# Odd mixer: three neighbouring pairs of steps change places in the order that TensorE follows

## Chip, cores and metric

The kernel runs on one core of a Trainium2 chip. The metric is the device time of one execution in microseconds (us), here the median of several executions. A profiled execution of the same kernel gives the trace from which all rows below come.

## What is computed

The reference is a two-layer network over 256 tokens of width 1024. Each layer has a gated feed-forward block, a mixer, a second feed-forward block and a gated per-layer embedding. The change concerns the mixer of the second layer, which the program calls `mix1`, the odd mixer:

```
x_gate, x_rg, u = split_cols(xn @ w_in, [512, 512, 512])
y_c = rg_lru_branch(x_gate, x_rg, ...)      # gated linear recurrence
y_d = s5_branch(u, ...)                     # state-space branch
h   = h + concatenate([y_c, y_d], axis=-1) @ w_out

rg_lru: xc = conv4(x_rg); r, i = sigmoid of two block-diagonal products of xc
        scan of (a, bx) over the tokens, times gelu(x_gate)
s5:     bu = B u;  x = complex scan of bu;  y = gelu(C x + d u)
        y * sigmoid(y @ w_glu + b_glu)
```

Everything is float32. Large products are made with three rounded matmuls (high x high, low x high, high x low), so that each weight tile is split into a rounded part `wh` and a rest `wl` before TensorE can use it.

## The kernel before

Activations are kept with features on the 128 partitions and the 256 tokens along the free axis. A projection of 1024 features into 128 is 8 steps of k with three matmuls each (lines 279, 280 and 281), 24 matmuls of 128x256, all into one PSUM tile `mm`. Weights come from DRAM through SyncE into `raw` tiles; ScalarE rounds them into `wh` (line 259), VectorE subtracts to get `wl` (line 260). `raw`, `wh` and `wl` have five buffers each, `mm` has five PSUM tiles, and `aux`, the PSUM tile of all small products, has three.

In the odd mixer a string, `ORDER`, lists steps by name and number. The program is written out step by step in that order, and TensorE (named PE in rows) executes its instructions in exactly this order (`manual_schedule` for PE). The instructions of VectorE (DVE), ScalarE (ACT), GpSimd (POOL) and SyncE (SP) are placed by a scheduler that follows from it. The steps that matter here:

- `r0` to `r3`: projections of the recurrence's input, 24 matmuls each. VectorE scales the result into `xr` (line 1205). `c` is the convolution (1212 on ScalarE, 1214 on VectorE), `b` its two gates (1224).
- `m0` to `m3`: matrices of one quarter of the S5 branch. Four transposes (line 1133) go into one `aux` tile, four more into a second, ScalarE copies both into `BT` (1134); then eight small products (1141) go into a third `aux` tile, `pk`, which VectorE (1142) and copies on both engines (1147) empty into `KT`.
- `s0` to `s3`: the states. Eight products (1157, tile `aux`) of the regrouped input `u4` (copied by both engines, line 1200) with `BT`; VectorE then works through lines 1160, 1161, 1163, 1164, two scans (1169), 1174, 1175, 1176 and 1177, which leave `XS`.
- `o0` to `o3`: the outputs. Products of `XS` and `u4` (1185, 1186) into one `aux` tile, which ScalarE empties with four Gelu activations (1188) into `us`.
- `z0`, `z2`: the product with `w_glu` (24 matmuls on tiles `BT`), then sigmoid on ScalarE (1265), a product on VectorE (1267), and a split of the result by ScalarE (304, `xhB`) and VectorE (305, `xlB`). `z0` gives parts 4 and 5 of the mixer's output `y`, `z2` parts 6 and 7.
- `p0` to `p3`: the first halves of four output projections, 12 matmuls each over parts 0 to 3 of `y`. The other halves, over parts 4 to 7, follow in `out_proj` directly behind the last step, beginning with output 0.

```
            steps = dict(
                s=s5_states, o=s5_out, m=s5_mats,
                r=lambda t: projected(xr[:, t, 3:], "r", t),
...
                z=glu,
                u=lambda q: self.ple_up(1, q),
                p=lambda j: self.out_first(y, j, ODD_HALF),
            )
            for st in ORDER.split():
                steps[st[0]](int(st[1:] or 0))
            self.out_proj(y, nxt, buf)
```

Of the kernel before, what the change touches and what calls it, by code (L numbers as in the profile page):

```python
# [61 lines left out]
CST = {}  # L62
M_SIDE = 1
F_SIDE = 16
ORDER = "r0 m0 s0 r1 m1 s1 o0 r2 m2 c0 o1 c1 r3 c2 c3 m3 b0 g0 b1 s2 b2 b3 s3 d g1 g2 g3 o2 e0 o3 y0 y2 e2 u0 h2 h0 f u1 z0 p0 p1 z2 p2 p3"
ODD_HALF = 0
RC_ENG = "vector"
EVEN_ORDER = "a x w0 w1 X Q0 d Q2 k Q4 Q6 K0 w2 V K2 e s0 q0 q1 l0 t0 w3 t1 l1 v0 t2 v1 t3 s4 v2 q2 o0 v3 o1 t4 q3 t5 t6 t7 v4 v5 u0 v6 v7 g y0 y2 u1 p0 p1 p2 p3"
# [140 lines left out]
class Kernel:  # L209
# [896 lines left out]
    def mix_odd(self, nxt, buf):  # L1106
# [6 lines left out]
        with ExitStack() as ctx:  # L1113
# [167 lines left out]
            )  # L1281
            for st in ORDER.split():
                steps[st[0]](int(st[1:] or 0))
# [118 lines left out]
```

## Time and profile before

| what | value |
|---|---|
| median of 3 runs | 1023.68 us (1023.31 to 1025.05) |
| the profiled execution's own time | 1031.07 us |
| its span from the first to the last instruction | 1029.3 us |
| mean granted TensorE clock over the span | 0.994 of full speed |
| busy: TensorE, VectorE, ScalarE, GpSimd | 98%, 73%, 56%, 5% of the span |

The profiled execution is 7.4 us longer than the median of the runs without a profile, and 1.8 us of it lie outside the span. The odd mixer stands at about 710 to 812 us of the span. In a row of a timeline the first number is the start from the beginning of the span, the second the busy time of all the instructions in the row; `[2.46 <-ACT BT L1134]` says that the engine stood idle for 2.46 us before it and what ended that. TensorE's starts are those at which matmuls issue: the busy time of a matmul overlaps the next one.

### The profile page before, as it was taken

The numbers are of one execution on the slowest core, as the hardware profiler recorded it, in microseconds if no ns is written. First come the engines' busy times: TensorE is split into PE (matmuls) and PEld (weight loads), VectorE is DVE, ScalarE is ACT, GpSimd is POOL, SyncE is SP. The second block draws the span as 40 slices with busy tenths as digits, with TensorE's granted clock in tenths as the row PEclk, the third lists the DMA queues.
The fourth block names the chain that finished last, engine by engine and source line by source line (L and its number), as shares of the span: only waits on it lengthen the run. The fifth ranks groups of instructions, "written<-read, shape, count | busy, mean of one in ns | idle before, by whom it ended". The sixth has DMA issues, their size and how long they took to land.

```text
span 1029.3 us, 21008 instructions
## 1 busy us (share of the span) xinstructions
PE 1009.5 (98%) x8526; PEld 994.3 (97%) x8526; DVE 753.1 (73%) x1350; ACT 571.4 (56%) x926; POOL 47.1 (5%) x134
## 2 busy tenths in 40 slices
PE   9999999999999999999999999999999999999996
PEld 8999999988899999999989999999898999999996
DVE  6877756589677777757689987876878777776665
ACT  7545445456565554546555764644678564545453
POOL 0000000200001000000240000002200000000000
PEclk9999999999999999999999999999899999999998
DMA  7655556465245655566446555564224565555641
GB/s 275 223 201 188 187 193 193 159 201 179 74 147 182 225 191 198 178 200 221 150 144 218 190 197 195 175 196 156 89 83 144 184 207 203 187 190 183 199 165 42
DMA packets 52945, 183.07 MB, mean 178 GB/s; under 512 B 5856, under 2 KB 6768, under 8 KB 52848
## 3 DMA queue, kind: packets, MB, share of 16 engines
q1 hardware_dynamic: 52160, 181.12, 52.7%
q8 instruction: 67, 1.10, 0.4%
q10 hardware_dynamic: 688, 0.61, 0.3%
q14 instruction: 30, 0.25, 0.1%
HBM read 180.13 MB, written 1.05 MB: 176 GB/s over the span
## 4 chain that ended last, share of the span: by engine, by line
PE 88%; DVE 6%; ACT 4%; issue 1%; DMA 1%; POOL 0%; SPq 0%; DVEq 0%; ACTq 0%; POOLq 0%
PE mm L279 26%; PE mm L281 26%; PE mm L280 26%; DVE wl L260 2%; ACT wh L259 1%; DMA h<-in_xT_dram 1%; PE mm L524 1%; PE mm L523 1%; PE mm L522 1%; PE mm L737 1%; PE mm L739 1%; PE mm L738 1%; PE aux L1141 0%; PE aux L1157 0%; PE aux L807 0%
## 5 line engine op out<-in xcount | busy, mean ns | idle before, releaser
L260 DVE TENSOR_TENSOR wl<-raw,wh 128x1024 fp32r<-128x1024 f32 (+2 forms) x350 | 414.8, 1190 | 152.0 <-ACT wh L259 151.4
L259 ACT CAST wh<-raw 128x1024 fp32r<-128x1024 f32 (+2 forms) x350 | 354.5, 1021 | 229.3 <-PE mm L280 108.0
L279 PE MATMUL mm<-xhA,wh 128*128 128x256 f32 x1200 | 331.8, 276 | 0.9 <-ACT xhA L322 0.9
L280 PE MATMUL mm<-xlA,wh 128*128 128x256 f32 x1200 | 332.0, 277 | 0.4
L281 PE MATMUL mm<-xhA,wl 128*128 128x256 f32 x1200 | 331.5, 276 | 0.0
L279 PEld LDWEIGHTS mm<-xhA,wh 128*128 128x128 f32 x1200 | 225.3, 188 | 1.6 <-ACT xhA L322 1.6
L280 PEld LDWEIGHTS mm<-xlA,wh 128*128 128x128 f32 x1200 | 225.3, 188 | 1.0 <-DVE xlA L323 1.0
L281 PEld LDWEIGHTS mm<-xhA,wl 128*128 128x128 f32 x1200 | 225.2, 188 | 0.2 <-DVE wl L260 0.2
L281 PE MATMUL mm<-gh,wl 128*128 128x256 f32 x704 | 195.2, 277 | 0.0
L279 PE MATMUL mm<-gh,wh 128*128 128x256 f32 x704 | 195.2, 277 | 0.0
L280 PE MATMUL mm<-gl,wh 128*128 128x256 f32 x704 | 195.2, 277 | 0.0
L281 PE MATMUL mm<-xhB,wl 128*128 128x256 f32 x576 | 162.1, 282 | 1.4 <-DVE wl L260 1.4
L279 PE MATMUL mm<-xhB,wh 128*128 128x256 f32 x576 | 162.6, 283 | 0.0
L280 PE MATMUL mm<-xlB,wh 128*128 128x256 f32 x576 | 162.2, 282 | 0.1
L281 PEld LDWEIGHTS mm<-gh,wl 128*128 128x128 f32 x704 | 132.9, 189 | 0.0
L280 PEld LDWEIGHTS mm<-gl,wh 128*128 128x128 f32 x704 | 132.1, 188 | 0.0
L279 PEld LDWEIGHTS mm<-gh,wh 128*128 128x128 f32 x704 | 132.1, 188 | 0.0
L281 PEld LDWEIGHTS mm<-xhB,wl 128*128 128x128 f32 x576 | 110.5, 192 | 1.7 <-DVE wl L260 1.6
L280 PEld LDWEIGHTS mm<-xlB,wh 128*128 128x128 f32 x576 | 109.4, 190 | 0.3 <-DVE xlB L305 0.3
L279 PEld LDWEIGHTS mm<-xhB,wh 128*128 128x128 f32 x576 | 109.2, 190 | 0.0
L304 ACT CAST gh<-s 128x256 fp32r<-128x256 f32 x88 | 35.4, 406 | 89.7 <-DVE s L416 89.7
L411 DVE TENSOR_TENSOR ab<-mm,R 128x512 f32<-128x512 f32 x82 | 56.4, 688 | 13.8 <-PE mm L281 12.6
(409 smaller groups left out, 1059.7 us busy)
## 6 DMA issues: line engine op xcount, KB each, us to landing
raw<-in_w_dram SPq DMA_DIRECT2D x309, 512.0 KB, 3.8
raw<-in_w_dram SPq DMA_DIRECT2D x36, 384.0 KB, 3.2
raw<-in_w_dram SPq DMA_DIRECT2D x4, 256.0 KB, 4.8
out_dram<-hg SPq DMA_DIRECT2D x4, 256.0 KB, 2.2
h<-in_xT_dram SPq DMA_DIRECT2D x2, 256.0 KB, 5.5
h<-in_xT_dram SPq DMA_DIRECT2D x1, 512.0 KB, 6.6
K<-kr ACTq DMA_DIRECT2D x2, 256.0 KB, 4.8
bd<-in_bd_dram SPq DMA_DIRECT2D x1, 512.0 KB, 4.6
```

Of the source, the lines that this page charges most:

```text
L259: nc.scalar.copy(wh[:, sl], raw[:, sl])
L260: self.last_split = nc.vector.tensor_sub(wl[:, sl], raw[:, sl], wh[:, sl].bitcast(F32))
L279: mm(out, wh, xh, start=start, stop=False)
L280: mm(out, wh, xl, start=False, stop=False)
L281: mm(out, wl, xh, start=False, stop=stop)
L304: self.nc.scalar.copy(hi, src)
L411: nc.vector.tensor_mul(ab, src[0].rearrange("p (t s) -> p t s", t=2), R[:, None, :].to_broadcast([P, 2, S]))
L522: mm(pt, a, wh, start=k == 0, stop=False)
L523: mm(pt, b, wh, start=False, stop=False)
L524: mm(pt, a, wl, start=False, stop=k == KD - 1)
L737: mm(pg[name][i], a, wh, start=k == 0, stop=False)
L738: mm(pg[name][i], b, wh, start=False, stop=False)
```

## The change

Three pairs of neighbours in `ORDER` change places: `s0 r1` becomes `r1 s0`, `o0 r2` becomes `r2 o0`, `z2 p2` becomes `p2 z2`.

```
-ORDER = "r0 m0 s0 r1 m1 s1 o0 r2 m2 c0 o1 c1 r3 c2 c3 m3 b0 g0 b1 s2 b2 b3 s3 d g1 g2 g3 o2 e0 o3 y0 y2 e2 u0 h2 h0 f u1 z0 p0 p1 z2 p2 p3"
+ORDER = "r0 m0 r1 s0 m1 s1 r2 o0 m2 c0 o1 c1 r3 c2 c3 m3 b0 g0 b1 s2 b2 b3 s3 d g1 g2 g3 o2 e0 o3 y0 y2 e2 u0 h2 h0 f u1 z0 p0 p1 p2 z2 p3"
```

No instruction is added or removed. TensorE's instructions move as blocks; those of the other engines move where the scheduler follows.

First place, TensorE behind `m0`. Before, these rows stand there (`aux_9416` is `m0`'s `pk`, `aux_9434` the tile of `s0`, `mm_9463` that of `r1`, `aux_9496` and `aux_9502` the two transposed tiles of `m1`; left out are further rows of the same tiles):

```order
L1141 MATMUL aux_9416<-cx_7221,xlA_7220 128x32
L1157 MATMUL aux_9434<-u_1376_9346,BT_9403 128x64 [waits DVE_49,Activation_49]
...
L279 MATMUL mm_9463<-xhB_8283,wh_9465 128x256
...
L1133 MATMUL aux_9496<-ident_76,xhA_7219 128x128 [waits PE_49]
...
L1133 MATMUL aux_9502<-ident_76,xlA_7220 128x128 [waits DVE_49,PE_49]
```

With the change (`aux_9466` is now the tile of `s0`, `mm_9434` that of `r1`):

```order
L1141 MATMUL aux_9416<-cx_7221,xlA_7220 128x32
L279 MATMUL mm_9434<-xhB_8283,wh_9436 128x256 [waits DVE_49,PE_49]
...
L1157 MATMUL aux_9466<-u_1376_9346,BT_9403 128x64 [waits DVE_49,Activation_49]
...
L1133 MATMUL aux_9496<-ident_76,xhA_7219 128x128 [waits PE_49]
...
L1133 MATMUL aux_9502<-ident_76,xlA_7220 128x128 [waits DVE_49,PE_49]
```

The projection `r1` has moved from behind `s0` to ahead of it, so that `m1` now follows `s0` directly. In the built program the second transposed tile of `m1` takes the PSUM bank that `s0` has just filled, and waits for VectorE's lines 1160 and 1161 to empty it. On VectorE these lines, with the emptying of `r1` ahead of them, stand as follows with the change:

```order
L260 TENSOR_TENSOR wl_9740<-raw_9738,wh_9739 128x1024 [waits DMAHW4_49,Activation_49]
L1205 TENSOR_TENSOR xr_9176<-mm_9434,R_9339 128x256 [waits PE_49]
L1147 COPY KT_1346_9172<-aux_9416 32x4x32 [waits Activation_49]
L1160 TENSOR_TENSOR ct_1399_9475<-aux_9466,rot_8648 128x512 [waits PE_49]
L1161 TENSOR_TENSOR ct_1400_9476<-aux_9466,rot_8648 128x512
```

Before, a third split of weights stood behind the one in the first row, and a copy of line 1147 between the last two rows; both have moved further down.

Second place, TensorE around `o0`. Before, `r2` (`mm_9572`) stood between `o0` (`aux_9555`) and `m2` (`aux_9605`, `aux_9611` and `pk` in `aux_9617`):

```order
L1186 MATMUL aux_9555<-u_1376_9346,KT_1346_9172 128x64
L279 MATMUL mm_9572<-xhB_8283,wh_9574 128x256
...
L1133 MATMUL aux_9605<-ident_76,xhA_7219 128x128 [waits DVE_49,PE_49]
...
L1133 MATMUL aux_9611<-ident_76,xlA_7220 128x128 [waits DVE_49,PE_49]
...
L1141 MATMUL aux_9617<-cx_7221,xhA_7219 128x32 [waits PE_49,Activation_49]
```

With the change `o0` is `aux_9587`, and `m2` follows it:

```order
L1186 MATMUL aux_9587<-u_1376_9346,KT_1346_9172 128x64
L1133 MATMUL aux_9605<-ident_76,xhA_7219 128x128 [waits DVE_49,PE_49]
...
L1133 MATMUL aux_9611<-ident_76,xlA_7220 128x128 [waits DVE_49,PE_49]
...
L1141 MATMUL aux_9617<-cx_7221,xhA_7219 128x32 [waits PE_49,Activation_49]
```

In both programs `pk` of `m2` takes the bank of `o0`, and its wait for ScalarE (`Activation_49`) is one for the Gelu activations of `o0`. What has moved is the projection between them.

Third place, ScalarE behind the epilogue of `z0`, with the change (`wh_10149` is the weight of `z2`, `wh_10192` that of `p3`, `wh_10287` that of output 4 in `out_proj`, `mm_10154` the tile of `z2`):

```order
L259 CAST wh_10149<-raw_10148 128x1024 [waits DMAHW7_49]
L259 CAST wh_10192<-raw_10191 128x1024 [waits DMAHW0_49]
L259 CAST wh_10287<-raw_10286 128x1024 [waits DMAHW1_49,DVE_49,PE_49]
L1265 ACTIVATE sq_10179<-mm_10154,cst_77 128x256 [waits PE_49]
L1265 ACTIVATE sq_10185<-mm_10154,cst_77 128x256
L304 CAST xhB_9369<-z_10181 128x256 [waits DVE_49]
```

Before, the rows stood in the same order, with the weight of `p2` in the first (the one of `z2` came earlier, in the place that `p2`'s has now). In both programs the third row waits until TensorE has done with the weight of `z2`, whose buffer it takes, and the sigmoids of `z2` stand behind it.

## Rows read from the trace of the kernel before

**Rows 1.** The page: each engine's busy time; the chain that ended last, by engine.

```profile
PE 1009.5 (98%) x8526; PEld 994.3 (97%) x8526; DVE 753.1 (73%) x1350; ACT 571.4 (56%) x926; POOL 47.1 (5%) x134
...
PE 88%; DVE 6%; ACT 4%; issue 1%; DMA 1%; POOL 0%; SPq 0%; DVEq 0%; ACTq 0%; POOLq 0%
```

**Rows 2.** TensorE's waits, whole span: us in total, times, longest.

```profile
PE aux L1157 <- ACT BT L1134: 2.5, 1, 2.5
PE mm L281 <- DVE wl L260: 2.2, 2, 1.4
```

**Rows 3.** Windows: length, then busy us (instructions) of PE, PEld, DVE, ACT, POOL, clock, DMA.

```profile
516.00:520.00 4.00, 2.66 (x24) 2.46 (x22) 4.00 (x9) 3.24 (x8) 1.00 (x1) 1.00 0.19 73
...
726.00:730.00 4.00, 3.74 (x18) 3.60 (x19) 3.09 (x5) 2.27 (x7) 2.87 (x1) 0.62 0.52 159
730.00:734.00 4.00, 4.00 (x22) 4.00 (x21) 3.53 (x8) 0.00 (x0) 0.40 (x1) 0.53 0.47 173
...
760.00:775.00 15.00, 15.00 (x128) 14.78 (x128) 14.68 (x26) 13.48 (x23) 1.45 (x3) 1.00 0.12 37
```

**Rows 4.** Timeline of TensorE, 726 to 746 us: `s0`, `r1`, `m1`, `s1`, `o0`, `r2`, `m2`.

```profile
726.21 3.55 PE L1157 MATMUL aux<-u,BT 128*128 128x64 f32 x16 [2.46 <-ACT BT L1134]
729.52 0.56 PE L279 MATMUL mm<-xhB,wh 128*128 128x256 f32 x1
...
734.34 0.60 PE L1133 MATMUL aux<-ident,xhA 128*128 128x128 f32 x4
...
736.91 1.98 PE L1157 MATMUL aux<-u,BT 128*128 128x64 f32 x16
738.73 0.61 PE L1185 MATMUL aux<-XS,cx 128*128 128x64 f32 x4
...
741.38 0.36 PE L279 MATMUL mm<-xhB,wh 128*128 128x256 f32 x1
...
744.29 0.60 PE L1133 MATMUL aux<-ident,xhA 128*128 128x128 f32 x4
...
745.16 0.31 PE L1141 MATMUL aux<-cx,xhA 128*128 128x32 f32 x2
```

**Rows 5.** Timeline of ScalarE, 725 to 745 us.

```profile
725.57 1.07 ACT L1134 COPY BT<-aux 128x512 f32<-128x512 f32 x2
...
741.65 1.28 ACT L1188 ACT_TABLE_LOAD   x1 [2.53 <-PE aux L1186]
742.95 1.54 ACT L1188 ACTIVATE us<-aux 32x256 f32<-32x256 f32 x4
```

**Rows 6.** Timeline of VectorE, 717 to 732 us.

```profile
717.91 2.36 DVE L260 TENSOR_TENSOR wl<-raw,wh 128x1024 fp32r<-128x1024 f32 x2 [1.32 <-ACT wh L259]
...
725.13 3.47 DVE L260 TENSOR_TENSOR wl<-raw,wh 128x1024 fp32r<-128x1024 f32 x3
...
729.80 0.69 DVE L1160 TENSOR_TENSOR ct<-aux,rot 128x512 f32<-128x512 f32 x1 [0.88 <-PE aux L1157]
...
730.60 0.68 DVE L1161 TENSOR_TENSOR ct<-aux,rot 128x512 f32<-128x512 f32 x1
```

**Rows 7.** Timeline of TensorE, 791 to 798 us: `z2`, then output 0.

```profile
791.20 0.38 PE L281 MATMUL mm<-BT,wl 128*128 128x256 f32 x1 [0.75 <-DVE wl L260]
...
793.77 0.28 PE L281 MATMUL mm<-BT,wl 128*128 128x256 f32 x1
...
797.76 0.39 PE L280 MATMUL mm<-xlB,wh 128*128 128x256 f32 x1
```

**Rows 8.** Timeline of ScalarE, 793 to 798 us.

```profile
793.97 1.05 ACT L259 CAST wh<-raw 128x1024 fp32r<-128x1024 f32 x1 [1.59 <-PE mm L280]
...
796.84 0.87 ACT L304 CAST xhB<-z 128x256 fp32r<-128x256 f32 x2 [1.08 <-DVE z L1267]
```

**Rows 9.** Timeline of VectorE, 791 to 798 us.

```profile
791.73 2.35 DVE L260 TENSOR_TENSOR wl<-raw,wh 128x1024 fp32r<-128x1024 f32 x2
795.05 1.23 DVE L260 TENSOR_TENSOR wl<-raw,wh 128x1024 fp32r<-128x1024 f32 x1 [0.97 <-ACT wh L259]
...
797.28 0.89 DVE L305 TENSOR_TENSOR xlB<-z,xhB 128x256 fp32r<-128x256 f32 x2
```

## Prediction

> **What bounds the kernel now.** I read the page first. TensorE is busy for 98% of the span and carries 88% of the chain that ended last [rows 1]. A change of order can therefore only win where TensorE stands still or runs slowly, and it loses where it makes TensorE wait. The list of TensorE's waits shows few: the longest of all is 2.5 us ahead of line 1157, behind ScalarE's copy of `BT` [rows 2], and this is the wait of `s0`. The windows of the granted clock come next: it is 0.62 in the mean from 726 to 730 us and 0.53 from 730 to 734 [rows 3], so TensorE ran at 1.2 in place of 2.4 GHz for about 7 us there, behind that wait. The timelines of the three engines around the three places give the durations. The reader is to see two things: a wait with a slow stretch behind it, which the first pair attacks, and three pieces of vector work (the emptying of `s0`, of `o0` and of `z2`) that lie under a projection now and do so no longer.
>
> **First pair, what it removes.** `s0` starts at 726.21 after 2.46 us of idle time, so `m0` ended at 723.75 [rows 4]. `r1` can start there: its weights are split at 717.91 + 2.36 = 720.27 [rows 6], in the same place on ScalarE and VectorE as before. A projection at full clock takes 744.29 - 741.38 = 2.91 us (`r2`), one at the low clock 734.34 - 729.52 = 4.82 us (`r1` now); the eight state products take 738.73 - 736.91 = 1.82 us (`s1`), those of `s0` now 729.52 - 726.21 = 3.31 [rows 4]. With the change `r1` runs from 723.75 to 726.66. `BT` is complete at 725.57 + 1.07 = 726.64 [rows 5], so `s0` follows at once and ends at 728.48. `m1` begins there and not at 734.34: 5.86 us earlier. Of these 2.46 are the wait, 1.49 + 1.91 = 3.40 the low clock, if the clock doesn't fall any more.
>
> **First pair, what it adds.** The second four transposes of `m1` need the bank of `s0`, so lines 1160 and 1161 must be done. Now `r1` lies between. VectorE began 1160 at 729.80, 0.28 us behind the start of the next matmul on TensorE, and the two lines take 0.69 and 0.68 [rows 4, 6]; the small copy between them moves behind. After the change that is 728.48 + 0.28 = 728.76 and an end at 730.13, or 0.1 sooner where the second begins before the first has written its last. VectorE is free by then: of its three splits from 725.13, 1.16 each, the third is moved away, so they end at 727.5, and the emptying of `r1` and a copy follow. The first transposes take half of 745.16 - 744.29 = 0.87 us [rows 4], so TensorE stands ready at 728.92 and waits **1.1 us** (1.0 to 1.3, the latter if the copy comes between all the same).
>
> **Second pair.** With `r2` ahead of it, `o0` stands 0.87 + 1.1 (the transposes and their wait) + 1.70 (the rest of `m1`, 736.91 - 734.34 - 0.87) + 1.82 (`s1`) + 2.91 (`r2`) = 8.4 us behind the end of `s0`; now it is 738.73 - 729.52 = 9.2 us without a wait [rows 4]. The move keeps that cover, and `o0`'s wait is 0 to 0.8 us; I take 0, since VectorE's chain from 1160 to `XS` has one wait on `r1` now that falls away. But `m2` loses its cover. Its `pk` needs the bank of `o0`, and ScalarE must first load the Gelu table and run four activations: they end at 742.95 + 1.54 = 744.49, which is 3.11 us behind the last of `o0` (741.38) [rows 4, 5]. Now `r2` fills that time. With the change only the eight transposes do, 0.87 us, so TensorE waits 2.2 us by the issue times; the first matmul of `r2` stands somewhat early in the model (its busy time is 0.36, that of the others 0.28), which takes 0.1 off: **2.1 us** (1.8 to 2.3). The table load starts only when `o0` is done (idle 2.53 us until then, released by line 1186 [rows 5]), so it cannot be hidden.
>
> A rule of the Trainium skill speaks against this pair more strongly: ScalarE: Activation LUTs, section What ACT_TABLE_LOAD costs, puts a switch to another set at 1283 ns and a drain of about 1380 ns. By it, which is an estimate from that page, the wait would be 2.1 + 1.4 = 3.5 us. The trace agrees with the load (1.28 us) but shows no drain behind it: the first Gelu starts 0.02 us after the load's end [rows 5]. The sum goes by the row.
>
> **Third pair.** `p2` comes into the place of `z2` and meets the same late split (0.75 us, [rows 7]): nothing changes there. `z2` follows twelve matmuls (half a projection, 1.45 us) later; its own `wl` is the first of the two at 791.73 and ready at 792.9 [rows 9], while `z2` needs it at 791.20 + 1.45 = 792.65: a wait of 0.25. The price lies behind `z2`. Its last matmul is at 793.77; then ScalarE splits the weight of output 4 (793.97), queued ahead of the sigmoids, VectorE does its half (795.05), and the split results come at 796.84 and 797.28, so that the matmul that needs part 6 starts at 797.76 [rows 7 to 9]. These 3.99 us hang on the end of `z2` alone. Now `p2`, `p3` and seven matmuls of output 0 cover all but 0.2 of it; with the change `p2` is gone from the cover, 1.45 us. Together **1.7 us** (1.4 to 1.9; ScalarE's and VectorE's order is the same, so nothing lets the sigmoids go first).
>
> **The sum.** 5.86 - 1.1 - 2.1 - 1.7 = 1.0 us earlier, and everything behind is a stream of matmuls that keeps the lead. By the bounds of these terms it is 0.4 (5.9 - 1.3 - 2.3 - 1.9) to 1.7 (5.9 - 1.0 - 1.8 - 1.4); a late `o0` would make it -0.4. The other queues cost nothing: SyncE's loads of `p2` and `z2` trade places under the three steps ahead of them, and GpSimd is busy for 5% [rows 1]. The profiled execution, 1031.07 us, would become 1030.1; the median of the runs is 7.4 us lower, and I assume that the difference carries over: 1023.68 - 1.0 = **1022.7**. A difference of 0.2%, 2.05 us, is about what can be told from none.
>
> **Rivals.**
> - The wait of `m2` makes the clock fall again (slower). For it: 2.1 us is close to the 2.46 us after which it fell, and what stands around both waits are small products and transposes. Against it: after the 1.4 us wait near 520 us [rows 2], with 1.34 us idle in its window, it stayed at 1.00 [rows 3]. It decides from a wait between 1.4 and 2.46 us on. Price, as for `s0` and `r1` now: 1.49 + 1.91 = 3.4 us, on `o1` and `r3`; 1023.68 - 1.0 + 3.4 = 1026.1, or 1024.4 if the low stretch is half as long. Chance 0.18.
> - The runs without a profile never had the slow stretch (slower). Only one execution shows it, and the three runs lie 1.7 us apart. Then 3.4 us of the saving don't exist: again 1026.1. Chance 0.13.
> - The third pair costs nothing, because output 0 can be kept busy or the splits come sooner than I follow them (faster): 1.0 + 1.7 = 2.7, so 1021.0. Against it: the order of ScalarE's rows. Chance 0.14.
> - VectorE becomes the bound: it is busy for 14.68 of the 15 us from 760 on [rows 3], and where it doesn't come earlier with TensorE, the lead of 2.7 is lost at `o3` and the third pair still costs 1.7: 1025.4. Against it: that full stretch begins behind `m3` and so moves with it. Chance 0.08.
> - The switch of the Gelu table holds ScalarE longer where TensorE waits for it. With as long again as the load itself, 1.28 us [rows 5], the sum is 1.0 - 1.3 = -0.3, so 1024.0. Against it: the row's activations follow the load at once. Chance 0.05. The page named above is what speaks for it.
>
> **How the numbers follow.** The forecast has 0.42 and its own range is 1021.9 to 1024.1. The range for 8 in 10 reaches from the free third pair, a little below (1020.6), to the two cases at 1026.1, a little above (1026.3); what is left out is a combination of two losses or a gain without any of the new waits. Faster by more than 0.2% (below 1021.63) is the free third pair and the edge of the forecast: 0.20. Slower (above 1025.73) is most of the first two rivals and some of the fourth: 0.26. The rest, 0.54, is within 0.2%.
>
> **What the profile of the changed kernel would show.** Right: no wait ahead of line 1157 at 726 us and a clock of 1.00 from 722 to 738; a wait of about 1.1 us ahead of the second transposes of `m1`, released by VectorE's 1161; one of about 2.1 us ahead of line 1141, released by ScalarE's 1188; `m3` about 2.7 us earlier than before; and about 1.6 us ahead of output 0's matmuls on parts 6 and 7, released by lines 304 and 305. Wrong: a clock of 0.5 anywhere from 730 to 750; no wait at 1141; output 0 running through; new waits at lines 1185 or 1224, which would be VectorE falling behind. The prediction fails as a whole if the slow stretch of before was not there in the timed runs, or comes back behind `m2`.

## The result, and the profile after

The changed kernel takes 1030.61 us (median of 7 runs, 1027.37 to 1032.68) against 1023.80 us of the kernel before beside it (7 runs, 1021.66 to 1025.50). The ratio is 1.0056 with a 95% interval of 1.0041 to 1.0070: slower by 0.56% (the medians lie 6.8 us apart), above the predicted range. Measured again beside other kernels it was 1029.82 against 1024.81, ratio 1.0056 (1.0035 to 1.0077).

The profiled execution of the changed kernel took 1027.37 us, its span is 1025.7. TensorE's waits over the whole span, to be held against [rows 2] (us in total, times, longest):

```profile
PE mm L281 <- DVE wl L260: 2.2, 2, 1.4
PE aux L1141 <- ACT us L1188: 2.1, 1, 2.1
...
PE mm L279 <- ACT xhB L304: 1.1, 1, 1.1
PE aux L1133 <- DVE ct L1161: 1.0, 1, 1.0
```

The 2.5 us ahead of line 1157 are gone, and three new waits stand there: `m2` behind the Gelus, output 0 behind the split of part 6, `m1` behind the emptying of `s0`. Where they stand is seen in TensorE's timeline, which answers to [rows 4] and [rows 7]:

```profile
721.20 2.14 PE L1157 MATMUL aux<-u,BT 128*128 128x64 f32 x16
...
724.82 0.63 PE L1133 MATMUL aux<-ident,xlA 128*128 128x128 f32 x4 [1.03 <-DVE ct L1161]
...
731.59 0.55 PE L1185 MATMUL aux<-XS,cx 128*128 128x64 f32 x4
...
734.21 0.61 PE L1133 MATMUL aux<-ident,xhA 128*128 128x128 f32 x4
...
737.34 0.41 PE L1141 MATMUL aux<-cx,xhA 128*128 128x32 f32 x2 [2.09 <-ACT us L1188]
...
739.15 0.87 PE L1185 MATMUL aux<-XS,cx 128*128 128x64 f32 x4
...
744.04 0.56 PE L279 MATMUL mm<-xhB,wh 128*128 128x256 f32 x1
...
747.89 0.60 PE L1133 MATMUL aux<-ident,xhA 128*128 128x128 f32 x4
...
794.63 0.38 PE L279 MATMUL mm<-xhB,wh 128*128 128x256 f32 x1 [1.12 <-ACT xhB L304]
```

`s0` starts without a wait, `o0` too. But behind the 2.09 us of `m2` everything becomes slow: `o1` takes 744.04 - 739.15 = 4.89 us, where `o0` took 734.21 - 731.59 = 2.62, and `r3` takes 747.89 - 744.04 = 3.85 us. The windows of the granted clock (length, then busy us and instructions of PE, PEld, DVE, ACT and POOL, the clock, the DMA share, GB/s) say why:

```profile
732.00:736.00 4.00, 3.25 (x30) 3.01 (x29) 4.00 (x9) 2.80 (x4) 1.73 (x3) 1.00 0.00 0
736.00:740.00 4.00, 2.66 (x21) 2.66 (x22) 1.40 (x5) 2.58 (x7) 0.26 (x2) 0.93 0.00 0
740.00:744.00 4.00, 4.00 (x21) 4.00 (x21) 3.84 (x10) 0.77 (x3) 0.83 (x2) 0.50 0.02 4
744.00:748.00 4.00, 4.00 (x28) 4.00 (x27) 1.17 (x2) 1.53 (x5) 0.04 (x1) 0.72 0.74 223
```

The clock is at 1.2 in place of 2.4 GHz for about 6.8 us ((0.07 + 0.50 + 0.28) x 4 / 0.5), as long as before behind the wait of `s0` [rows 3], some 12 us later in the span, or 18 us later in the mixer, which began 5.2 us earlier in this execution (line 387 ahead of it: 712.61 against 717.81 us). A second low stretch, of 3.4 us, stands at 258 us, in the even mixer, where no instruction was moved (two windows, same columns):

```profile
256.00:260.00 4.00, 4.00 (x26) 3.64 (x25) 2.16 (x5) 0.84 (x3) 0.00 (x0) 0.77 0.75 220
260.00:264.00 4.00, 4.00 (x20) 3.19 (x20) 0.79 (x2) 2.00 (x3) 0.00 (x0) 0.81 0.11 44
```

One more difference concerns the profile of before, not the change. In the second feed-forward block the same projection matmuls stood closer together in the changed kernel's execution. First before, then after, the same 60 us at full clock:

```profile
580.00:640.00 60.00, 60.00 (x512) 60.00 (x511) 49.21 (x89) 35.56 (x59) 0.00 (x0) 1.00 0.57 194
```

```profile
580.00:640.00 60.00, 60.00 (x532) 60.00 (x531) 51.02 (x97) 36.88 (x62) 0.00 (x0) 1.00 0.63 201
```

512 against 532 instructions: start to start 0.1178 against 0.1133 us. Summed over all projection matmuls, the slower step cost the profiled execution of before 9.6 us and that of after 1.3. These 8.3 us account for the 7.4 us by which the profile of before lay over its median.

### The profile page after: what moved, and what is told of

It reads as the page before. It is cut to its first block, busy times and chain, and to the rows that moved or that the text cites. A ratio compares the mean times of both kernels' runs of the same rounds, so it can differ in the third digit from the quotient of the medians.

```text
span 1025.7 us, 21005 instructions
## 1 busy us (share of the span) xinstructions
PE 1003.5 (98%) x8526; PEld 987.0 (96%) x8526; DVE 752.0 (73%) x1350; ACT 571.5 (56%) x926; POOL 45.9 (4%) x134
## 4 chain that ended last, share of the span: by engine, by line
PE 89%; DVE 6%; ACT 3%; issue 1%; DMA 1%; POOL 0%; SPq 0%; DVEq 0%; ACTq 0%; POOLq 0%
PE mm L279 26%; PE mm L281 26%; PE mm L280 26%; DVE wl L260 2%; ACT wh L259 1%; PE aux L1141 1%; DMA h<-in_xT_dram 1%; PE mm L524 1%; PE mm L522 1%; PE mm L523 1%; PE mm L737 1%; PE mm L739 1%; PE mm L738 1%; PE aux L1157 1%; PE aux L1185 0%
## 5 line engine op out<-in xcount | busy, mean ns | idle before, releaser
L281 PE MATMUL mm<-xhB,wl 128*128 128x256 f32 x576 | 159.8, 278 | 2.2 <-DVE wl L260 2.2
L279 PE MATMUL mm<-xhB,wh 128*128 128x256 f32 x576 | 160.3, 278 | 1.3 <-ACT xhB L304 1.1
L280 PE MATMUL mm<-xlB,wh 128*128 128x256 f32 x576 | 159.6, 277 | 0.1
```

Of the source, the lines that this page charges most:

```text
L279: mm(out, wh, xh, start=start, stop=False)
L280: mm(out, wh, xl, start=False, stop=False)
L281: mm(out, wl, xh, start=False, stop=stop)
```

## The experiments

Three theories. Theory 1: the time was lost inside the odd mixer, to the new waits and to a clock that falls behind them. Theory 2, its rival: it was lost in stretches that the change doesn't touch (258 us, the step of the matmuls). Theory 3 came out of the first four runs: the clock falls where little is computed, in the waits and in the small products around them. All runs are compared with the kernel before on the same chip: 1024.03 us for the first four, 1024.81 for the others.

**The kernel before, unchanged**, to see what differs between executions.

> The kernel before, unchanged, profiled a second time, because its first profile was 7.4 us longer than its median and shows two steps between matmuls in a row: 0.1133 us in most stretches, 0.118 us from 531 to 718 and from 784 to 826 us, 9.6 us in all. Theory 1 (the change costs what it does to the waits and the clock inside the odd mixer): median 1023 to 1025, and the slower step is chance: another stretch, or none, this time. Theory 2 (the times differ because of stretches that the change doesn't touch): the same program's own executions lie 5 us or more apart, and their clocks differ as those of the changed kernel did (0.988 to 0.992).

1025.53 us, ratio 1.0011 (0.9999 to 1.0023). Its profile has a low stretch behind `s0`'s wait again, but 3.4 us long and not 6.8. The slow step of the matmuls was there again (8.5 us), and it is in the profile of the first pair alone (8.8 us); the other ten profiles have 1.3 to 2.9 us of it. In these three most of it lies between 520 and 718 us, where no kernel here moves an instruction, so it isn't the change that brings it.

**The three pairs apart.** First pair:

```
-r0 m0 s0 r1 m1 s1 o0 r2 m2
+r0 m0 r1 s0 m1 s1 o0 r2 m2
```

> The first pair alone (r1 ahead of s0). Theory 1: 5.9 us saved at s0 and r1, 1.1 us lost at m1's second transposes and about 0.5 us ahead of o0, no wait of 2 us at m2 and so no fall of the clock in the mixer: 4 us under the kernel before, about 1019.7. Theory 2: no clear difference, within 2 us of the kernel before.

1025.21 us, ratio 1.0016 (1.0001 to 1.0031): a miss, since the pair that was to save most saved nothing. `s0`'s wait is gone, and the waits left are short (timeline of TensorE, `m1`, `o0` and `r2`):

```profile
731.63 0.63 PE L1133 MATMUL aux<-ident,xlA 128*128 128x128 f32 x4 [1.03 <-DVE ct L1161]
...
736.49 1.09 PE L1185 MATMUL aux<-XS,cx 128*128 128x64 f32 x4 [0.70 <-DVE XS L1176]
...
741.60 0.56 PE L279 MATMUL mm<-xhB,wh 128*128 128x256 f32 x1
...
746.70 0.60 PE L1133 MATMUL aux<-ident,xhA 128*128 128x128 f32 x4
```

Yet `o0` takes 5.11 us and `r2` 5.10: the clock is 0.53 from 736 to 740 us, 0.50 from 740 to 744 and 0.69 from 744 to 748, a low stretch of 10.2 us, longer than the one that was removed. This execution is the slowest of the twelve (1032.74 us; it has the slow step of the matmuls as well), and its mean granted clock, 0.989, is among their lowest: the others have 0.989 to 0.994, so a low stretch of this length isn't shown for all of them.

```profile
736.00:740.00 4.00, 3.52 (x17) 3.55 (x17) 3.97 (x10) 0.17 (x1) 0.00 (x0) 0.53 0.00 0
740.00:744.00 4.00, 4.00 (x20) 4.00 (x20) 2.00 (x4) 2.04 (x4) 0.89 (x3) 0.50 0.00 0
744.00:748.00 4.00, 4.00 (x28) 4.00 (x26) 1.08 (x3) 1.93 (x4) 0.00 (x0) 0.69 0.00 0
```

Second pair:

```
-r0 m0 s0 r1 m1 s1 o0 r2 m2
+r0 m0 s0 r1 m1 s1 r2 o0 m2
```

> The second pair alone (r2 ahead of o0). Theory 1: the wait of 2.5 us at s0 stays, the wait of about 2.1 us at m2's line 1141 comes, and the clock can fall behind both (3.4 us each): 2.1 to 5.5 us over the kernel before, 1026 to 1029. Theory 2: within 2 us of the kernel before.

1032.73 us, ratio 1.0087 (1.0070 to 1.0104): worse than expected. Both waits are there, 2.5 us at `s0` and 2.1 at `m2`, and a low stretch of 10.2 us at each: the first begins inside `s0`'s wait, at 718.25 us, the second behind `m2`'s, at 742.15.

Third pair:

```
-z0 p0 p1 z2 p2 p3
+z0 p0 p1 p2 z2 p3
```

> The third pair alone (p2 ahead of z2). Theory 1: 1.7 us over the kernel before, about 1025.5, with about 1.6 us of waits ahead of output 0's parts 6 and 7, and no fall of the clock there. Theory 2: within 1 us of the kernel before.

1026.83 us, ratio 1.0018 (1.0006 to 1.0029): slower, as expected, by 1.8 to 2.8 us as one takes the ratio or the medians. The wait ahead of output 0 is 1.1 us, as in the changed kernel.

**The clock alone.** The next two kernels shorten no wait. They put a product of a matrix of ones with itself, some twenty times, into it, so that TensorE computes while it waits; the results are overwritten. In the changed kernel, ahead of `m2`'s second transposes:

```
                     pt = self.aux()
+                    for _ in range(18 if b == 2 and i == 1 else 0):
+                        nc.tensor.matmul(pt[:, :S], self.ones_r[:, :P], self.ones_r, start=True, stop=True)
```

> This is the changed kernel with 18 products of a matrix of ones with itself (128x256, 0.113 us each by the step of a projection, 2.04 us in all, their results overwritten) put between the first and the second transposes of m2, inside the wait of 2.09 us ahead of line 1141. Nothing is taken off the path: line 1141 still starts when line 1188 is done. Theory 3 (the clock falls where TensorE computes little, in the waits and in the small products around them; what a wait costs in the clock is lost even if the wait itself cannot be shortened): the granted clock stays at 1.00 from 736 to 748 us, o1 takes 2.7 us in place of 4.9 and r3 2.75 in place of 3.85, and the time is 3.3 us below that of the changed kernel, 1027.3 us. Rival (the clock falls by the small products themselves, whatever stands in the wait): the low stretch is there all the same, perhaps later, and the time is 1030 to 1031.

1025.23 us, ratio to the kernel before 1.0014 (0.9980 to 1.0047), where the changed kernel has 1.0056. Its profile has a span of 1020.8 us, 4.9 below that of the changed kernel, and no low stretch between 12 and 1014 us. Of the 4.9 us, 3.1 lie in the odd mixer and 1.6 at 258 us, far ahead of the filling. The twelve runs spread from 1022.5 to 1035.3 us, and the two intervals still overlap (1.0047 and 1.0041 are their near ends); the mean granted clock of the twelve is 0.9938, that of the changed kernel run again 0.9898. TensorE's timeline at `m2`, `o1`, `r3` and `m3` (lines are two higher here):

```profile
732.95 2.39 PE L1133 MATMUL aux<-ones 128*128 128x256 f32 x18
...
735.72 0.41 PE L1143 MATMUL aux<-cx,xhA 128*128 128x32 f32 x2
...
737.52 0.64 PE L1187 MATMUL aux<-XS,cx 128*128 128x64 f32 x4
...
740.20 0.36 PE L279 MATMUL mm<-xhB,wh 128*128 128x256 f32 x1
...
743.12 0.60 PE L1135 MATMUL aux<-ident,xhA 128*128 128x128 f32 x4
```

`o1` takes 2.68 us, `r3` 2.92, against 4.89 and 3.85 with the same wait left empty. The 1.03 us of `m1` were not filled and did no harm.

In the kernel before, ahead of `s0` (the tile is that of `r1`, allocated early):

```
+                if b == 0:
+                    early.append(self.psum()[:, :S])
+                    for _ in range(20):
+                        nc.tensor.matmul(early[0], self.ones_r[:, :P], self.ones_r, start=True, stop=True)
```

> This is the kernel before with 20 products of a matrix of ones with itself (128x256, 2.27 us by the step of a projection, results overwritten by r1) put ahead of s0, inside its wait of 2.46 us. s0 still starts when line 1135's second copy of BT is done. Theory 3: the granted clock stays at 1.00 from 726 to 734 us, s0 takes 1.82 us in place of 3.31 and r1 2.91 in place of 4.82, 3.4 us less: 1020.6 us against 1024.0 of the kernel before. Rival (small products alone): a low stretch behind m1, s1 and o0 in its place, 1023 to 1025. Second rival (the timed runs of before have no low stretch, so that nothing can be won back): 1024.0.

1022.06 us, ratio 0.9975 (0.9951 to 0.9998): faster than the kernel before with one useless stretch of work more, by an interval that only just leaves out 1. The mean granted clock of its runs is 0.9958, of the kernel before beside it 0.9926. In its profile, of span 1018.2, no low stretch is left but at its two ends. The filling, `s0` (line 1163 here), `r1` and `m1`:

```profile
716.68 2.63 PE L1159 MATMUL mm<-ones 128*128 128x256 f32 x20
719.38 2.26 PE L1163 MATMUL aux<-u,BT 128*128 128x64 f32 x16
721.46 0.36 PE L279 MATMUL mm<-xhB,wh 128*128 128x256 f32 x1
...
724.26 0.60 PE L1133 MATMUL aux<-ident,xhA 128*128 128x128 f32 x4
```

`s0` takes 2.08 us (1.82 expected) and `r1` 2.80, against 3.31 and 4.82 in [rows 4]. The filling didn't delay `s0`: it starts 0.64 us behind the start of ScalarE's copies of `BT` (719.38 - 718.74), as in the kernel before (726.21 - 725.57, [rows 4, 5]).

**First and second pair without the third:**

```
-z0 p0 p1 p2 z2 p3
+z0 p0 p1 z2 p2 p3
```

> The changed kernel without its third pair (z2 stays ahead of p2). By the step of the prediction the third pair costs 1.7 us, by the run of it alone 1.8 to 2.8 us (1026.83 against 1024.03). Theory 3: the low stretch behind m2's wait is there as in the changed kernel and only the wait ahead of output 0's matmuls goes, 1028 to 1029 us. Rival (the costs of the pairs don't add up, since a later start leaves the third pair more or less cover): 1030.6 or 1027.

1026.60 us, ratio 1.0015 (0.9987 to 1.0043), lower than the expected 1028 to 1029; single runs at a lower clock reach 1032 and more. The profile shows `m2`'s wait of 2.1 us, the low stretch of 6.8 us behind it and the one at 258 us, and no wait ahead of output 0.

**The first pair with its two waits filled** (8 products of ones in `m1`, 5 ahead of `o0`, over the first pair alone):

```
                     pt = self.aux()
+                    if b == 1 and i == 1:
+                        fill(8)
...
             def s5_out(b):
                 kt = KT[b % 2]
+                if b == 0:
+                    fill(5)
```

> The first pair alone, with products of ones (128x256, results overwritten by r2) in its two waits: 8 (0.91 us) between the first and second transposes of m1, where it waits 1.03 us for line 1161, and 5 (0.57 us) ahead of o0, where it waits 0.70 us for line 1176. No wait gets shorter. Without them the profiled execution ran at the low clock from 736.24 for 10.24 us, from o0 on. Theory 3 (the waits between the small products bring the clock down): it stays at 1.00 from 720 to 750 us, o0 takes 2.7 us in place of 5.1 and r2 2.8 in place of 5.1, and the first pair shows what the prediction asked of it: 5.86 - 1.1 - 0.7 = 4.1 us below the kernel before, 1020.2 us where before is 1024.3. Rival (four groups of small products in a row, s0 m1 s1 o0, bring it down whatever stands between them): a low stretch from 736 us all the same, 1024.5 to 1025.5.

1022.05 us, ratio 0.9985 (0.9970 to 1.0001), and the twelve runs come in two kinds. Seven have a mean granted clock of 0.996 to 0.998, and six of these take 1020.00 to 1020.95 us, as theory 3 had it. Five have 0.989 to 0.992 and take 1023.2 to 1026.4, nearer the rival. The profile is of the second kind: the clock falls although no wait is left among the small products, at the end of `s1` (timeline of TensorE, `s1`, the filling, `o0`, `r2`; lines are 11 and 13 higher):

```profile
725.65 1.98 PE L1168 MATMUL aux<-u,BT 128*128 128x64 f32 x16
727.43 1.34 PE L1133 MATMUL mm<-ones 128*128 128x256 f32 x5
728.57 0.95 PE L1198 MATMUL aux<-XS,cx 128*128 128x64 f32 x4
...
733.54 0.56 PE L279 MATMUL mm<-xhB,wh 128*128 128x256 f32 x1
```

```profile
724.00:728.00 4.00, 4.00 (x36) 4.00 (x36) 3.37 (x8) 1.60 (x5) 1.80 (x3) 0.94 0.04 16
728.00:732.00 4.00, 4.00 (x21) 4.00 (x21) 3.97 (x10) 0.02 (x1) 0.00 (x0) 0.50 0.00 0
```

Neither theory alone holds: groups of small products in a row, with the products of ones between them, are enough in some executions, and in others they are not.

**Another order, with more projections between the groups of small products:**

```
-r0 m0 s0 r1 m1 s1 o0 r2 m2 c0 o1 c1 r3 c2 c3 m3
+r0 m0 r1 s0 r2 m1 s1 o0 r3 m2 c0 o1 c1 c2 c3 m3
```

> The kernel before with another order of the recurrence: r0 m0 r1 s0 r2 m1 s1 o0 r3 m2 c0 o1 c1 c2 c3 m3, then as before. A projection stands between every two groups of small products up to o1, s0 doesn't wait, m1's second transposes find line 1161 done under r2, m2's line 1141 finds line 1188 done under r3; by the durations of before the waits left are about 0.5 us ahead of m3's line 1141 and 1.3 us at the split of xg. Theory 3: no low stretch from 715 to 745 us, or one of 3.4 us at the most, and 3.4 us less waiting than the kernel before (2.46 ahead of s0, about 1 in the third projection), less the 1.8 of new waits: 5.8 - 1.8 = 4 us below before, 1020 us. Theory 1 (waits alone) gives a gain too, of 0.6 (2.46 - 1.8) plus the clock. Rival (o1, c, m3 with no projection in between are now the row of small products): the clock falls there, 1023 to 1024.

1021.67 us, ratio 0.9968 (0.9946 to 0.9990). Its profile (span 1017.2) has no low stretch in the odd mixer, and the longest waits there are 0.8 us at `m3`'s line 1141 and 1.1 ahead of line 280. The expectation overstates the order in one point: `m1`, `s1` and `o0` still stand in a row, without a wait, and so do `m2`, `o1` and `m3`.

The same with `z2` earlier:

```
-z0 p0 p1 z2 p2 p3
+z0 p0 z2 p1 p2 p3
```

> The order of e6_spread with z2 one output earlier (z0 p0 z2 p1 p2 p3 in place of z0 p0 p1 z2 p2 p3), so that p1, p2 and p3 stand behind z2 and cover the splits for output 4. The cover grows by half a projection, 1.45 us, but the wait that it still has to cover is 0.2 us and z2 itself then meets its own weights sooner. Theory (the third pair's price, the cover behind z2, works in the other direction too): 0.2 to 0.5 us below e6_spread, so 3.3 to 3.6 below the kernel before, 1020.8 us where before is 1024.3. Rival (nothing left to cover there): 3.1 below, as e6_spread, or a new wait of z2 that makes it 2.5 below.

1019.79 us (1019.48 to 1020.43), ratio 0.9957 (0.9945 to 0.9969): the fastest kernel of all, faster than both. Its profile caught one low stretch, 3.4 us at 744 us, behind `m3`'s wait, where `m2`, `o1` and `m3` stand in a row:

```profile
741.67 0.41 PE L1141 MATMUL aux<-cx,xhA 128*128 128x32 f32 x2 [0.75 <-ACT us L1188]
```

```profile
744.00:748.00 4.00, 4.00 (x21) 3.87 (x20) 3.94 (x6) 1.75 (x6) 0.00 (x0) 0.57 0.34 110
```

What `z2` itself adds to the gain is not settled: 1.9 us by the medians (of two chips), while in the profiles this order is 0.7 us ahead once its low stretch is taken off (next section), against 0.2 to 0.5 expected.

**The changed kernel again:**

> The changed kernel again, unchanged, beside the others on one chip, for a second look at where its clock falls. Theory 3: the low stretch behind m2's wait (3.4 to 10 us long) is there again, and the low stretch near 258 us, where the program is that of before, only by chance. In time 1026.1 (the prediction with the clock's fall behind m2's wait, its first rival) plus one or two more low stretches at 1.6 us each: 1028 to 1031 where before is 1024. Rival (the first measurement was high because of the chip or the hour): 1026 or less.

1029.82 us, ratio 1.0056 (1.0035 to 1.0077). Both low stretches are where they were, 3.4 us at 258 and 6.8 us at 739. The first measurement was no accident of its chip.

## Why the prediction was wrong

The odd mixer can be timed apart: from the first row of line 387 ahead of it to the first of the next stage, which in the two filled kernels stand at (after with the wait filled, then before with the wait filled)

```profile
710.89 0.28 PE L387 MATMUL aux<-frame,ms 128*128 128x256 f32 x1
...
817.34 0.28 PE L387 MATMUL aux<-frame,ms 128*128 128x256 f32 x1
```

```profile
710.92 0.28 PE L387 MATMUL aux<-frame,ms 128*128 128x256 f32 x1
...
814.81 0.28 PE L387 MATMUL aux<-frame,ms 128*128 128x256 f32 x1
```

that is, 106.45 and 103.89 us. All thirteen profiled executions, measured so, with the low clock inside the stretch as the trace's record of the clock gives it, and the slow matmul step where it costs over 1 us (behind the stretch every span has another 203.4 to 203.5 us):

| kernel | odd mixer, us | low clock in it, us, and where it begins |
|---|---|---|
| before | 108.07 (1.6 of it the slow matmul step) | 6.8 at 727 |
| before, again | 105.48 | 3.4 at 728 |
| before, wait filled | 103.89 | none |
| after | 109.57 | 6.8 at 739 |
| after, again | 109.72 | 6.8 at 739 |
| after, wait filled | 106.45 | none |
| first pair | 108.08 | 10.2 at 736 |
| first pair, waits filled | 108.16 | 10.2 at 728 |
| second pair | 115.78 (1.5 slow step) | 10.2 at 718, 10.2 at 742 |
| third pair | 109.92 (1.5 slow step) | 6.8 at 720 |
| first and second pair | 108.79 (1.4 slow step) | 6.8 at 740 |
| projections between | 102.55 | none |
| the same, `z2` earlier | 103.45 | 3.4 at 744 |

**The waits were sized rightly.** `m1`: 1.1 predicted, 1.03 measured. `m2`: 2.1 predicted, 2.09 measured. `o0`: none, as chosen. Third pair: 1.7 predicted. At full clock 106.45 - 103.89 = 2.56 us separate the two orders, and with the 2.46 that fell away and the 1.03 and 2.09 that came, 2.56 + 2.46 - 1.03 - 2.09 = 1.9 are left for it. Two rows show where it went (changed kernel with the wait filled):

```profile
783.77 0.38 PE L281 MATMUL mm<-BT,wl 128*128 128x256 f32 x1 [0.15 <-DVE wl L260]
...
789.78 0.38 PE L279 MATMUL mm<-xhB,wh 128*128 128x256 f32 x1 [1.13 <-ACT xhB L304]
```

From start to start, `z2`'s matmul of the first row stands 0.43 us behind the one before it, where 0.12 is usual. That of output 0 in the second row stands 1.41 us behind its predecessor, and the next one 0.46 behind it; the kernel before with its wait filled has 0.11 and 0.33 there. That is 0.31 + 1.30 + 0.13 = 1.7 us, as predicted. Without the clock, then, the prediction's own terms make the change cost 1.1 + 2.1 + 1.7 - 2.46 = 2.4 us, and 2.56 were measured.

**The step that failed** is the condition on the 3.40 us: "if the clock doesn't fall any more". It fell. The 3.40 themselves were near: before against before filled is 108.07 - 103.89 less the 1.1 us by which their slow steps differ, 3.05 us. But after against after filled is 109.57 - 106.45 = 3.12 us. The change took the low stretch away behind `s0` and laid one of the same length and price behind `m2`, one of the two ways in which, by its own words, the prediction "fails as a whole". In sum +2.56 and not -1.0: that alone would be 1023.7 + 2.6 = 1026.3, the edge of the range.

**The first rival had the mechanism** (the wait of `m2` brings the clock down, 3.4 us, 1026.1) and deserved the largest chance and not 0.18. Its condition was read wrongly, though. I took the length of the wait as what decides, somewhere between 1.4 and 2.46 us. The first pair alone brought the clock down with waits of 1.03 and 0.70 us, and with these filled it still fell in some executions. The 1.4 us at 520 us that spoke against it [rows 2, 3] stand among projections, where it stayed at 1.00; the prediction had named the small products around the other waits, and counted them as the lesser sign.

**The rest of the loss is clock too, by the means of the runs.** The timed runs of the changed kernel had more of it than its profile. Where the changed kernel was run again, the mean granted clock is 0.9898 over six runs, and 0.9924 over the 17 of before. That is 0.0026 x 1027 / 0.5 = 5.3 us more at 1.2 GHz, at 3.12 / 6.8 = 0.46 us each 2.4 us. With the 2.56 this makes 5.0; the means of the two differ by 1029.6 - 1024.3 = 5.3. Where in the span those runs were slow no trace shows. For the first measurement, with 6.8 us between the medians and 6.1 between the means, the clock of before's runs is not at hand, and 1 to 2 us of it stay unexplained. A part of the clock's loss lies outside the change: the low stretch at 258 us is in four of the thirteen profiles (after, after again, first pair, first and second pair) and costs 1.6 us there (122.68 us from line 387 to line 387 where the others have 121.10). The instructions up to it are the same in all these orders. All four kernels' orders have the first pair, but something else sets these executions apart: by the trace's record, the clock first rose to 1.00 at 5.5 to 5.9 us of the span in these four, and at 4.2 to 4.9, at 6.3 to 6.9 or at 10.7 us in the other nine. So the stretch at 258 us goes with the moment at which the clock rose at the kernel's start, which lies ahead of the change. Why it does, no run here shows.

**The other rivals.** The runs without a profile did have the slow stretch: filling it made the kernel before 2.75 us faster in the median. The third pair was not free. VectorE did not become the bound: no wait stands ahead of lines 1185 or 1224. The switch of the Gelu table held nothing longer; ScalarE's timeline of the changed kernel:

```profile
734.46 1.28 ACT L1188 ACT_TABLE_LOAD   x1 [1.19 <-PE aux L1186]
735.75 1.54 ACT L1188 ACTIVATE us<-aux 32x256 f32<-32x256 f32 x4
```

The first Gelu follows 0.01 us behind the load, as in [rows 5], now that TensorE waits for it. The Trainium skill (ScalarE: Activation LUTs, section What ACT_TABLE_LOAD costs) adds a drain of about 1380 ns to each switch; the trace has its 1.28 us of load and no drain, and the wait came out at the row's 2.09 us and not at 3.5. The theory that the time was lost outside the odd mixer explains 1.6 us of the profile and none of the difference between filled and unfilled kernels.

**The base was unsafe as well.** The sum started from one execution and assumed that its 7.4 us over the median carry over. They were the slower matmul step, and all but 1.6 us of that lies outside the mixer. What should have been asked of that one profile is how long the low stretch is in other executions: 6.8 us in it, 3.4 in the next one of the same kernel.

## What to carry to other kernels

A saving that is half wait and half low clock is two terms: the wait is gone when the order is changed, the clock only if nothing of the new order brings it down again, and that is to be asked of every place where small products meet, not only of the longest wait. Where such a wait can't be shortened, products that nobody needs can be put into it (20 of them made the kernel before 0.25% faster); better is an order that breaks the row of small products by projections and leaves no long wait (0.32% faster, 0.43% with `z2` earlier). Two or three profiled executions of the same kernel show what belongs to it and what to the execution, which one profile cannot.

## What was not expected of the hardware

- The same 128x256 matmuls follow each other at 0.1133 us in most stretches and at 0.1178 in others, at a granted clock of 1.00 and without waits, over 187 us in the profile of before (531 to 718 us). Three of the thirteen profiles have it there (before twice, 9.6 and 8.5 us in all, and the first pair, 8.8 us), though no kernel here moves an instruction in that stretch; what brings it stays open.
- The clock fell with no wait to start it: in the first pair with filled waits at 727.5 us, behind `m1` and `s1`, when TensorE had not been idle for over 0.2 us since `m0`. In the same kernel seven of twelve runs kept a mean clock of 0.996 or more. The Trainium skill (TensorE: Matmul & The Clock Gate, Part 1) calls the number of slow matmuls at a kernel's start run-variable; here the low stretches in the middle of the kernel are, too: 3.4 or 6.8 us in the two profiles of before.
